# Expert routing on 64 candidate sums in place of 256, with norm sums and side steps reordered

## The chip, the cores and the metric

The kernel runs on one core of one Trainium2 chip. The metric is the device time of one execution in microseconds (us), the median of several runs. Durations of single instructions come from one profiled execution. Engines are called PE (matrix multiplication), DVE (vector), ACT (scalar), POOL (GpSimd) and SP (which issues DMAs).

## The reference, cut to what matters

A two-layer network over 256 tokens of width 1024, all in 32-bit floats. The first layer ends in a feed-forward part with product keys; the change is mostly there:

```
q = (ht @ w_q).reshape(T, PEER_HEADS, PEER_QDIM)
s1 = jnp.einsum('thd,nd->thn', q[..., :PEER_HALF], sub_k1)
s2 = jnp.einsum('thd,nd->thn', q[..., PEER_HALF:], sub_k2)
v1, i1 = lax.top_k(s1, PEER_TOPK)
v2, i2 = lax.top_k(s2, PEER_TOPK)
cand = (v1[..., :, None] + v2[..., None, :])      # 16 x 16 sums
cand_idx = (i1[..., :, None] * PEER_NKEYS + i2[..., None, :])
vals, pos = lax.top_k(cand, PEER_TOPK)
experts = jnp.take_along_axis(cand_idx, pos, axis=-1)
gates = jax.nn.softmax(vals, axis=-1)
```

There are 8 heads; each token and head chooses 16 of 128 x 128 = 16384 experts, whose rows `expert_u` and `expert_v` then weigh into the output. The kernel computes the products with all experts densely and masks them, so all of `expert_u` and `expert_v` streams through PE.

## The kernel before, in words

**Tiling.** Tokens are two tiles of 128 (`NT`). Weights come from HBM in blocks of 128 x 1024 floats (`w`, issued by SP). Each block is split into a high part on ACT (`whi`, line 298) and a low part on DVE (`wlo`, line 307), and a product is three matmuls (lines 408 to 410): one by the low part of the activations, one high by high, one by `wlo`. A block of `p_u`, `p_wq` or the like takes 24 matmuls of 256 columns.

**Buffers.** There are four buffers for `whi` and three for `wlo`; `prefetch` splits ahead as far as these reach. So a `wlo` may start only when PE has ended the block three before it, and DVE, which works in program order, stands still until then with all that is queued behind it.

**Side work.** Routing, norms and rotary steps are generators in the list `side`. After each block `tick` runs the steps that `after(n, f)` has put n ticks ahead, and then lets generators go on until `pace` credits are spent; a step costs what it yields (`STEP`, 650, where it yields nothing). `finish()` runs all that is left in `side` at once. The order of instructions on every engine is thus fixed when the program is written out.

**Routing.** `route` runs beside two stages: the query projection `p_wq` (16 blocks) and the first half of the experts' `p_u` (64 blocks, `u_pair`, outputs in `A1`). For each head and token tile `top16` chooses twice from 128 scores (lines 1227 to 1232: the best eight, their places, striking them out, and the same again), then POOL forms the 256 sums `cand` (line 1302), and `pick` chooses 16 of them. `keys(q)` turns the chosen places into indices of experts for four heads: `rr`, `rf` are row and column of the place, `eq` compares them with 0 to 15 (1024 wide), a product on POOL (line 1277) and a sum on DVE (line 1288) give `i1s`, `i2s`. `keys(0)` runs beside heads 5 to 7, `keys(1)` after the last head; behind it the gates are normalized (lines 1308 to 1314), and six transposes on PE (line 1320) bring indices and gates into place. The loop over `p_u` is followed by `finish()`.

**Norms.** `nm.columns` sums squares on PE (line 490) and starts the root (line 495 on DVE, 496 on POOL); `squares` and `diagonal` (502, 503, 514) prepare the matrix that PE spreads to rows (line 523).

**Second layer.** The attention pairs `pair_scores` and `full_flip` (lines 1753 and 1678) run with side steps of the last query slab (`q1`, `qkv_steps`); the pooling stage (line 2049) adds its products to `xT`.

Of the kernel before, what the change touches and what calls it, by code (L numbers as in the profile page):

```python
# [21 lines left out]
FT = mybir.dt.float32  # L22
# [128 lines left out]
def body(tc, a, out, dbg=None):  # L151
# [84 lines left out]
    with top:  # L236
# [419 lines left out]
        with b1:  # L656
# [37 lines left out]
            low_next()  # L694
            nm.square(2)
            nm.square(3)
            after(5, nm.squares)
            after(5, nm.diagonal)
            after(6, nm.rows)
            cb1 = ap_.tile([64, 512], FT, name="c_c_b1")  # L700
            cb2 = ap_.tile([16, 128], FT, name="c_c_b2")
# [124 lines left out]
                return evac_steps(lambda t, o: q_steps(name, dst, gain, t, o), ready[name])  # L826

            k_evac = evac_steps(k_steps, ready["ak"])
            kv_evac_ = evac_steps(kv_steps, ready["kk"])

            def kv_evac(t, o):
                if t == 0:
                    nm.columns()
                kv_evac_(t, o)

            def v_evac(t, o):
                S.activation(av[:, t], o, AF.Copy, scale=nm.rc[:, t:t + 1])
# [396 lines left out]

        KEYLAG = 8

        def route():
            def buf(dt, n):
                return [rp2.tile([128, 8, 16], dt, name=n, tag=n) for t in range(NT)]

            v12 = [buf(FT, f"v{e}") for e in range(2)]
            i12 = [buf(U32, f"i{e}") for e in range(2)]
            if12 = [buf(FT, f"if{e}") for e in range(2)]
            vals, pos = buf(FT, "vals"), buf(U32, "pos")
            last = [None, None]

            def pick(h, t):
                yield from top16(vals[t][:, h], pos[t][:, h], last[t].rearrange("p a b -> p (a b)"), 256)

            def keys(q):  # L1250

                hs, ks = ts(q, 4), ts(q, 64)
                for t in range(NT):
                    for e in range(2):
                        V.tensor_copy(if12[e][t][:, hs], i12[e][t][:, hs])
                    rr = rp2.tile([128, 2, 64], U32, name="rr", tag="rr", bufs=1)
                    rf = rp2.tile([128, 2, 64], FT, name="rf", tag="rf", bufs=2)
                    pf = pos[t][:, hs].rearrange("p h k -> p (h k)")
                    V.tensor_scalar(rr[:, 0], pf, 4, None, op0=OP.logical_shift_right)
                    V.tensor_scalar(rr[:, 1], pf, 15, None, op0=OP.bitwise_and)  # L1260
                    V.tensor_copy(rf, rr)
                    V.tensor_tensor(ig[2][:, t, ks].rearrange("p (h k) -> p h k", h=4), vals[t][:, hs],
                                    vals[t][:, hs, 0:1].to_broadcast([128, 4, 16]), op=OP.subtract)
                    yield
                    for e in range(2):
                        eq = rp2.tile([128, 4, 16, 16], FT, name="eq", tag="eq", bufs=2)
                        ef = eq.rearrange("p h k r -> p (h k) r")
                        args = (ef, rf[:, e, :, None].to_broadcast([128, 64, 16]), iota[:, None, 0:16].to_broadcast([128, 64, 16]))
                        if q == 0:

                            G.tensor_tensor(*args, op=OP.subtract)
                            S.activation(eq, eq, AF.Square)
                            S.activation(eq, eq, AF.Relu, scale=-1.0, bias=1.0)
                        else:
                            V.tensor_tensor(*args, op=OP.is_equal)
                            yield 1200
                        G.tensor_tensor(eq, eq, if12[e][t][:, hs, None, :].to_broadcast([128, 4, 16, 16]), op=OP.mult)
                        yield 1 if q == 0 else None
                        if q == 0:
                            w = 8  # L1280
                            while w > 1:
                                G.tensor_tensor(ef[:, :, 0:w], ef[:, :, 0:w], ef[:, :, w:2 * w], op=OP.add)
                                w //= 2
                            G.tensor_tensor(ig[e][:, t, ks, None], ef[:, :, 0:1], ef[:, :, 1:2], op=OP.add)
                            for _ in range(KEYLAG):
                                yield 1
                        else:
                            V.tensor_reduce(ig[e][:, t, ks], ef, axis=AX.X, op=OP.add)
                            yield 1200

            for h in range(8):
                while heads[0] <= h:
                    yield
                if h == 5:
                    spawn(keys(0))
                for t in range(NT):
                    for e in range(2):
                        yield from top16(v12[e][t][:, h], i12[e][t][:, h], sc[t][:, h, e], 128)
                    if h:
                        yield from pick(h - 1, t)  # L1300
                    last[t] = rp2.tile([128, 16, 16], FT, name="cand", tag="cand")
                    G.tensor_tensor(last[t], v12[0][t][:, h, :, None].to_broadcast([128, 16, 16]),
                                    v12[1][t][:, h, None, :].to_broadcast([128, 16, 16]), op=OP.add)
            for t in range(NT):
                yield from pick(7, t)
            yield from keys(1)

            S.activation(ig[2], ig[2], AF.Exp)
            gs = rp2.tile([128, 2, NT * 8], FT, name="gs", tag="gs", bufs=1)
            gall = ig[2].rearrange("p t (h k) -> p (t h) k", k=16)  # L1310
            V.tensor_reduce(gs[:, 0], gall, axis=AX.X, op=OP.add)
            V.tensor_scalar(gs[:, 0], gs[:, 0], 1.0 / GATE, None, op0=OP.mult)
            V.reciprocal(gs[:, 1], gs[:, 0])
            V.tensor_tensor(gall, gall, gs[:, 1, :, None].to_broadcast([128, NT * 8, 16]), op=OP.mult)
            yield
            yield
            g3 = [bank("tp"), bank("tp")]
            for i in range(3):
                for t in range(NT):
                    tr(g3[i // 2][:, ts((i % 2) * 2 + t)], ig[i][:, t], ident)  # L1320
            for i in range(2):
                V.tensor_copy(ib[i], g3[0][:, ts(i, T)])
            yield

            gT = g3[1][:, 0:T]
            V.tensor_copy(gp2[0], gT)
            V.tensor_tensor(gp2[1], gT, gp2[0], op=OP.subtract)

        pace[0] = 1 * STEP
        after(4, nm.columns)  # L1330
        after(5, nm.diagonal)
        after(6, nm.rows)
# [24 lines left out]
        def u_pair(c):  # L1357
            u_leave(c, u_products(c))

        pace[0] = 1200  # L1360
        o = u_products(0)
        head_scores(7)
        rs.close()
# [252 lines left out]
        with ExitStack() as es:  # L1616
            yp = pool(es, "y", side="right")
            y = yp.tile([128, 4, 512], FT, name="y")
            ws = [get("p_v", 126), get("p_v", 127, more=False)]

            def last_mm(q):
                h, t = divmod(q, 2)
                for k in range(2):
                    v_mm(126 + k, ws[k], t, (h,))

            def leave(q):
                if q == 1:
                    V.tensor_scalar(y[:, q], acc[q], 1.0 / GATE, None, op0=OP.mult)
                else:
                    S.activation(y[:, q], acc[q], AF.Copy, scale=1.0 / GATE)  # L1630

            def turned(h):
                o = [bank("tp") for _ in range(2)]
                for t in range(NT):
                    for i in range(4):
                        tr(o[i // 2][:, (i % 2) * T + t * 128:(i % 2) * T + (t + 1) * 128], y[:, 2 * h + t, ts(i)], ident)
                for k in range(2):
                    add(2 * h + k, o[k])

            for q in range(3):  # L1640
                last_mm(q)
                leave(q)
            turned(0)
            last_mm(3)
            leave(3)
            nm.operand(0)
            nm.operand(1)
            prefetch(3)
            filled(1)
            turned(1)  # L1650
            nm.operand(2)
            prefetch(2)
            nm.operand(3)
            prefetch(3)
            last_squares(nm)

        def full_scores(s, stk, scale, bufs):
# [25 lines left out]
        with at:  # L1683
# [82 lines left out]
            for pr in range(8):  # L1766
                if pr == 3:
                    finish(slab_steps[1])
                if pr < 7:
                    ss = pair_scores(pr + 1)  # L1770
                pts = []
# [8 lines left out]
                if pr < 7:  # L1780
                    pp = pair_probs(ss, pr + 1)
                if pr == 0:
                    q1.unit(3)

                kfs[0].tag = "s" if pr in (1, 2) else "mm"
                filled(FILL["pairs"][pr])
# [225 lines left out]
        with pm:  # L2012
# [23 lines left out]
            for gp_ in range(2):  # L2036
                w = get("pool", gp_)
                for q in range(2):
                    g = 2 * gp_ + q
                    o = bank()  # L2040
                    for d in range(2):
                        for k in range(2):
                            c0 = (2 * q + k) * 256 + d * 128
                            mm3(o[:, ts(d, T)], cut(w, ALL, slice(c0, c0 + 128)), cut(mT, ALL, 2 * g + k), k == 0, k == 1)
                    if g >= 2:
                        prefetch()
                    for d in range(2):
                        c = 2 * g + d
# [69 lines left out]
```

## Time and profile before

| | us |
|---|---|
| median of 3 runs (1732.07 to 1736.66) | 1734.8 |
| the profiled execution | 1734.57 |
| its span in the trace | 1732.8 |
| PE busy in the span | 1706.4 |
| DVE busy | 1377.5 |
| ACT busy | 941.9 |
| POOL busy | 164.4 |

PE is busy nearly all the time, so the few stretches in which it waits, or runs at a lower granted clock, are what side work can change. The span leaves 1.8 us of the profiled execution outside; the profiled execution stands 0.2 us below the median. Ends of matmuls are modelled, and two that follow each other overlap in the records: a matmul of 256 columns shows 0.28 us, while the next starts 0.12 us after it.

### The profile page before, as it was taken

To read this page: it belongs to the slowest core of one execution; us is meant where nothing else is said; L and a number is where in the kernel's file an instruction comes from. 1 tells how busy PE (TensorE), PEld (TensorE's weight loads), DVE (VectorE), ACT (ScalarE), POOL (GpSimd) and SP (SyncE) were. 2 spreads that over 40 slices of the span, in tenths; PEclk is the share of its full clock that TensorE was granted. 3 is DMA by queue.
4 is the path that set the end of the run, shared out by engine and by line. 5 is a ranking of instruction groups with operands and counts; after the bars stand their busy time and mean duration, and the time that the engine had idled before them with its cause. 6 is when DMAs were issued, how large, how long until landed. Compare 5 with 4: busy or idle time off the path is not lost. (4 is left out here: it accounts for less than half of the span.)

```text
span 1732.8 us, 31970 instructions
## 1 busy us (share of the span) xinstructions
PE 1706.4 (98%) x12658; PEld 1559.9 (90%) x12658; DVE 1377.5 (79%) x2440; ACT 941.9 (54%) x1399; POOL 164.4 (9%) x123
## 2 busy tenths in 40 slices
PE   9999999999999999999999999999999999999998
PEld 8977999999999998888888888689999999899997
DVE  6888879999877887898766658876788877678786
ACT  6556556445544444444454555665666666556664
POOL 1210020155200000000010001010200001020000
PEclk9999999999999999999999999999999999999999
DMA  6633455555655555555655655244656554455653
GB/s 233 204 119 101 135 177 176 188 169 170 197 177 167 168 169 183 170 171 169 216 190 187 195 165 183 86 146 134 198 184 204 186 179 157 135 188 192 188 189 122
DMA packets 83238, 297.66 MB, mean 172 GB/s; under 512 B 9280, under 2 KB 10320, under 8 KB 82960
## 3 DMA queue, kind: packets, MB, share of 16 engines
q1 hardware_dynamic: 81360, 291.68, 52.0%
q0 software_dynamic: 608, 2.62, 0.4%
q8 instruction: 99, 1.62, 0.4%
q10 hardware_dynamic: 1120, 1.32, 0.2%
q14 instruction: 51, 0.42, 0.1%
HBM read 294.54 MB, written 1.05 MB: 171 GB/s over the span
## 5 line engine op out<-in xcount | busy, mean ns | idle before, releaser
L298 ACT ACTIVATE whi<-w 128x1024 fp32r<-128x1024 f32 x537 | 566.1, 1057 | 437.2 <-PE s L1476 160.4
L307 DVE TENSOR_TENSOR wlo<-w,whi 128x1024 fp32r<-128x1024 f32 x537 | 682.7, 1276 | 129.7 <-issue 52.7
L410 PE MATMUL s<-hT,wlo 128*128 128x256 f32 x1024 | 286.7, 280 | 3.3 <-DVE wlo L307 3.2
L408 PE MATMUL s<-hT,whi 128*128 128x256 f32 x1024 | 287.4, 281 | 0.0
L409 PE MATMUL s<-hT,whi 128*128 128x256 f32 x1024 | 286.2, 280 | 0.0
L1476 PE MATMUL mm<-whi,hT 128*128 128x512 f32 x762 | 234.9, 389 | 0.0
L410 PEld LDWEIGHTS s<-hT,wlo 128*128 128x128 f32 x1024 | 191.9, 187 | 4.7 <-DVE wlo L307 4.6
L408 PEld LDWEIGHTS s<-hT,whi 128*128 128x128 f32 x1024 | 192.2, 188 | 0.0
L409 PEld LDWEIGHTS s<-hT,whi 128*128 128x128 f32 x1024 | 192.1, 188 | 0.0
L1476 PEld LDWEIGHTS mm<-whi,hT 128*128 128x128 f32 x762 | 143.0, 188 | 30.1
L1476 PE MATMUL mm<-wlo,hT 128*128 128x512 f32 x381 | 129.7, 394 | 0.0
L408 PE MATMUL mm<-hT,whi 128*128 128x256 f32 (+1 forms) x360 | 102.7, 285 | 0.0
L410 PE MATMUL mm<-hT,wlo 128*128 128x256 f32 (+1 forms) x360 | 101.7, 283 | 0.0
L409 PE MATMUL mm<-hT,whi 128*128 128x256 f32 (+1 forms) x360 | 101.4, 282 | 0.0
L408 PE MATMUL tp<-xTl,whi 128*128 128x256 f32 x352 | 99.6, 283 | 0.0
L408 PE MATMUL s<-xTl,whi 128*128 128x256 f32 x352 | 98.9, 281 | 0.0
L409 PE MATMUL s<-xTh,whi 128*128 128x256 f32 x352 | 98.8, 281 | 0.0
L410 PE MATMUL s<-xTh,wlo 128*128 128x256 f32 x352 | 98.8, 281 | 0.0
L410 PE MATMUL tp<-xTh,wlo 128*128 128x256 f32 x352 | 98.8, 281 | 0.0
L409 PE MATMUL tp<-xTh,whi 128*128 128x256 f32 x352 | 98.8, 281 | 0.0
L1476 PE MATMUL s<-whi,hT 128*128 128x512 f32 x254 | 98.5, 389 | 0.0
L397 DVE TENSOR_TENSOR hT<-A,hT 128x512 fp32r<-128x512 f32 (+1 forms) x64 | 44.0, 688 | 61.1 <-ACT hT L396 60.5
(478 smaller groups left out, 3957.9 us busy)
## 6 DMA issues: line engine op xcount, KB each, us to landing
w<-in_p_u_dram SPq DMA_DIRECT2D x128, 512.0 KB, 3.3
w<-in_p_v_dram SPq DMA_DIRECT2D x128, 512.0 KB, 3.4
w<-in_f_up_dram SPq DMA_DIRECT2D x88, 512.0 KB, 3.3
w<-in_f_down_dram SPq DMA_DIRECT2D x44, 512.0 KB, 3.9
w<-in_p_wq_dram SPq DMA_DIRECT2D x16, 512.0 KB, 3.3
w<-in_x_k_dram SPq DMA_DIRECT2D x16, 512.0 KB, 3.6
w<-in_x_v_dram SPq DMA_DIRECT2D x16, 512.0 KB, 3.4
w<-in_x_q_dram SPq DMA_DIRECT2D x16, 512.0 KB, 3.5
```

The lines of the kernel that those rows point to most:

```text
L298: S.activation(hi[:, c], w[:, c], AF.Copy)
L307: V.tensor_sub(lo[:, c], w[:, c], hi[:, c].bitcast(FT))
L397: V.tensor_sub(lo, src, hi.bitcast(FT))
L408: mm(o, l[0], r[1], start=start, stop=False, **kw)
L409: mm(o, l[0], r[0], start=False, stop=False, **kw)
L410: mm(o, l[1], r[0], start=False, stop=stop, **kw)
L1476: mm(acc[2 * h + t], l[k], w[m][:, ts(h, 512)], start=c == 0 and k == 0 and m == 1, stop=c == 127 and k == 1)
```

## The change

1. **64 sums.** With both lists sorted, a sum at row a and column b can be among the best 16 only where (a+1)(b+1) is at most 16. `cand` now holds four rectangles of the 16 x 16 table (`STAIRS`: row 0 with 16 columns, rows 1 to 3 with 8, rows 4 to 7 with 4, rows 8 to 15 with 1), 64 places, formed by four POOL instructions; `pick` runs over 64. `keys` must turn a place among 64 into row and column, which takes ten more small DVE instructions for each of its four passes, and one more `yield`.
2. **Pace.** `pace` is 1000 in place of 650 in `p_wq`, and 720 in place of 1200 in `p_u`.
3. **First norm.** `columns` goes from the evacuation `kv_evac` to a tick later, ahead of `squares` and `diagonal`.
4. **Squares before attention.** `prefetch(3)` becomes `prefetch()`, so one more `wlo` is issued there.
5. **Attention pairs.** `pace` is 0 around `q1.unit(3)`, `STEP` until pair 3, and then `2 * STEP`.
6. **Pooling.** `prefetch()` is called for g = 3 alone, not for g = 2.

```diff
+            for f in (nm.columns, nm.squares, nm.diagonal):
+                after(5, f)
...
+        STAIRS = ((0, 1, 16, 0), (1, 4, 8, 16), (4, 8, 4, 40), (8, 16, 1, 56))
...
-                yield from top16(vals[t][:, h], pos[t][:, h], last[t].rearrange("p a b -> p (a b)"), 256)
+                yield from top16(vals[t][:, h], pos[t][:, h], last[t], 64)
...
+                    row = rf[:, 0]
+                    V.tensor_scalar(row, rw[:, 0], -1.0, 0.0, op0=OP.add, op1=OP.max)
+                    V.scalar_tensor_tensor(row, rw[:, 1], -6.0, row, op0=OP.add, op1=OP.max)
+                    V.scalar_tensor_tensor(row, rw[:, 2], -48.0, row, op0=OP.add, op1=OP.max)
...
+                    V.tensor_tensor(rf[:, 1], rw[:, 2], rw[:, 0], op=OP.subtract)
+                    yield
...
+                    last[t] = rp2.tile([128, 64], FT, name="cand", tag="cand")
+                    for i0, i1, m, p0 in STAIRS:
+                        G.tensor_tensor(last[t][:, p0:p0 + (i1 - i0) * m].rearrange("p (a b) -> p a b", b=m),
+                                        v12[0][t][:, h, i0:i1, None].to_broadcast([128, i1 - i0, m]),
+                                        v12[1][t][:, h, None, 0:m].to_broadcast([128, i1 - i0, m]), op=OP.add)
...
-        pace[0] = 1 * STEP
+        pace[0] = 1000
...
-        pace[0] = 1200
+        pace[0] = 720
...
-            prefetch(3)
+            prefetch()
...
+                    pace[0] = 0
                     q1.unit(3)
+                    pace[0] = STEP
...
-                    if g >= 2:
+                    if g == 3:
                         prefetch()
```

The rows below are the order in which instructions stand on an engine; numbers behind a name tell buffers apart, and the numbers of lines above 680 differ between the two kernels.

DVE at the kernel's first norm, before: `nst` at line 495 takes the sums from PE, and `qn` at line 760 is the rotary work on the first products.

```order
L484 TENSOR_TENSOR nacc<-nacc 128x256
L307 TENSOR_TENSOR wlo<-w,whi 128x1024
L495 TENSOR_SCALAR nst<-tp 128x2
L760 TENSOR_TENSOR qn<-mm,c_ghead 128x128 x4
L307 TENSOR_TENSOR wlo<-w,whi 128x1024
L502 TENSOR_SCALAR nst<-nst 128x2
L503 TENSOR_TENSOR nst<-nst 128x2
L514 TENSOR_TENSOR ndg<-first,nst 128x256
```

And after the change:

```order
L484 TENSOR_TENSOR nacc<-nacc 128x256
L307 TENSOR_TENSOR wlo<-w,whi 128x1024
L760 TENSOR_TENSOR qn<-mm,c_ghead 128x128 x4
L307 TENSOR_TENSOR wlo<-w,whi 128x1024
L495 TENSOR_SCALAR nst<-tp 128x2
L502 TENSOR_SCALAR nst<-nst 128x2
L503 TENSOR_TENSOR nst<-nst 128x2
L514 TENSOR_TENSOR ndg<-first,nst 128x256
```

`nst` of line 495, and with it POOL's root, has moved behind the four `qn` and a `wlo`. On PE the two matmuls of line 490 stand 24 matmuls (one block) later.

DVE at the end of the first half of `p_u`, before: the last token tile of `keys(1)` and the gates, from its first comparison to the casts of the transposed results.

```order
L1275 TENSOR_TENSOR eq_5606<-rf_5601,c_iota_2835 128x1024
L307 TENSOR_TENSOR wlo_5610<-w_5506,whi_5572 128x1024
L307 TENSOR_TENSOR wlo_5641<-w_5539,whi_5614 128x1024
L1288 TENSOR_REDUCE i1s_2837<-eq_5606 128x64
L307 TENSOR_TENSOR wlo_5674<-w_5570,whi_5645 128x1024
L1275 TENSOR_TENSOR eq_5704<-rf_5601,c_iota_2835 128x1024
L307 TENSOR_TENSOR wlo_5706<-w_5612,whi_5678 128x1024
L307 TENSOR_TENSOR wlo_5739<-w_5643,whi_5710 128x1024
L1288 TENSOR_REDUCE i2s_2838<-eq_5704 128x64
L307 TENSOR_TENSOR wlo_5770<-w_5676,whi_5743 128x1024
L1311 TENSOR_REDUCE gs_5801<-gts_2839 128x16
```

And after the change, from the last `wlo` ahead of the same work (between `i2s` of the first tile and the first `eq` here lie sixteen instructions 64 or 128 wide of lines 1252 to 1274):

```order
L307 TENSOR_TENSOR wlo_5957<-w_5865,whi_5931 128x1024
L1300 TENSOR_REDUCE i2s_2838<-eq_5923 128x64
...
L1287 TENSOR_TENSOR eq_6009<-rf_5994,c_iota_2835 128x1024
L1300 TENSOR_REDUCE i1s_2837<-eq_6009 128x64
L1287 TENSOR_TENSOR eq_6013<-rf_5994,c_iota_2835 128x1024
L1300 TENSOR_REDUCE i2s_2838<-eq_6013 128x64
L1327 TENSOR_REDUCE gs_6018<-gts_2839 128x16
L1328 TENSOR_SCALAR gs_6018<-gs_6018 128x16
L1329 RECIPROCAL gs_6018<-gs_6018 128x16
L1330 TENSOR_TENSOR gts_2839<-gts_2839,gs_6018 128x256
L1338 CAST ib0_2831<-tp_6023 128x256
```

Where six `wlo` stood between these steps, none stands now: they are written out in one piece by `finish()`.

PE at the same place, after the change: the last matmul of the block that uses `wlo_5893`, the transposes, and the first of the next block. (`wlo_5863` is used by the block before; `wlo_5957` takes its buffer.)

```order
L410 MATMUL s_5926<-hT_2840,wlo_5893 128x256
L1336 MATMUL tp_6023<-first_76,i1s_2837 128x128 x2
L1336 MATMUL tp_6023<-first_76,i2s_2838 128x128 x2
L1336 MATMUL tp_6024<-first_76,gts_2839 128x128 x2
L408 MATMUL s_6056<-hT_2840,whi_5897 128x256
L410 MATMUL s_6056<-hT_2840,wlo_5927 128x256
```

Before, the transposes stood three blocks (72 matmuls) earlier, inside the loop; now they stand behind its last block.

## Rows read from the trace of the kernel before

**Rows 1.** Page, part 1: busy us, share of the span, instructions.

```profile
PE 1706.4 (98%) x12658; PEld 1559.9 (90%) x12658; DVE 1377.5 (79%) x2440; ACT 941.9 (54%) x1399; POOL 164.4 (9%) x123
```

**Rows 2.** Timeline of PE, one block of p_u: start us, us, instruction.

```profile
453.91 0.28 PE L408 MATMUL s<-hT,whi 128*128 128x256 f32 x1
...
456.73 0.28 PE L408 MATMUL s<-hT,whi 128*128 128x256 f32 x1
```

**Rows 3.** Waits of PE over the span: us in total, times, longest us.

```profile
PE s L410 <- DVE wlo L307: 3.2, 4, 1.4
PE tp L490 <- DVE nacc L484: 2.1, 1, 2.1
PE s L1753 <- ACT fp L1664: 1.8, 3, 1.0
PE mm L408 <- DVE xT L2049: 1.2, 1, 1.2
...
PE mm L408 <- DVE wlo L307: 0.9, 1, 0.9
...
PE tp L1320 <- DVE gts L1314: 0.3, 1, 0.3
```

**Rows 4.** Windows: length, then busy (x) of PE, PEld, DVE, ACT, POOL, then PEclk.

```profile
21.60:23.20 1.60, 1.60 (x10) 1.60 (x9) 0.00 (x0) 1.44 (x3) 0.11 (x1) 0.51 0.92 246
23.20:25.00 1.80, 1.80 (x11) 1.80 (x10) 1.55 (x5) 1.80 (x5) 0.00 (x0) 0.50 0.26 100
```

**Rows 5.** Timeline at the first norm: start us, us, engine, line, [idle before <-releaser].

```profile
19.70 0.61 PE L490 MATMUL tp<-ones,nacc 128*128 128x2 f32 x4 [2.09 <-DVE nacc L484]
...
21.00 0.71 POOL L496 TENSOR_TENSOR nst<-nst,nhalf 128x2 f32<-128x2 f32 x1 [18.30 <-DVE nst L495]
...
24.35 1.22 DVE L307 TENSOR_TENSOR wlo<-w,whi 128x1024 fp32r<-128x1024 f32 x1
...
25.76 0.42 DVE L514 TENSOR_TENSOR ndg<-first,nst 128x256 f32<-128x256 f32 x1
...
27.50 0.61 PE L523 MATMUL tp<-ndg,ones 128*128 128x128 f32 x4
```

**Rows 6.** Timeline near the end of p_wq: a wlo, and its first use.

```profile
277.29 1.21 DVE L307 TENSOR_TENSOR wlo<-w,whi 128x1024 fp32r<-128x1024 f32 x1
...
279.92 0.28 PE L410 MATMUL s<-hT,wlo 128*128 128x256 f32 x1
```

**Rows 7.** Timeline in p_u: POOL's product, the wlo beside it, PE.

```profile
369.33 2.40 POOL L1277 TENSOR_TENSOR eq<-eq,if 128x1024 f32<-128x1024 f32 x1 [2.77 <-ACT eq L1273]
369.40 3.41 DVE L307 TENSOR_TENSOR wlo<-w,whi 128x1024 fp32r<-128x1024 f32 x1
...
372.87 0.39 PE L410 MATMUL s<-hT,wlo 128*128 128x256 f32 x1 [1.41 <-DVE wlo L307]
```

**Rows 8.** Groups of DVE by form: count, busy us, mean ns, idle before.

```profile
L1227 DVE MAX8 v<-sc 128x8 f32<-128x128 f32 x32 | 9.0, 280 | 0.0
...
L1227 DVE MAX8 vals<-cand 128x8 f32<-128x256 f32 x16 | 6.6, 413 | 0.0
...
L1275 DVE TENSOR_TENSOR eq<-rf,c_iota 128x1024 f32<-128x1024 f32 x4 | 4.9, 1216 | 0.0
...
L1255 DVE CAST if<-i 128x64 f32<-128x64 uint32 x8 | 1.1, 182 | 0.0
```

**Rows 9.** Timeline of DVE at the end of routing.

```profile
454.72 1.21 DVE L1288 TENSOR_REDUCE i2s<-eq 128x64 f32<-128x1024 f32 x1
...
457.57 0.42 DVE L1311 TENSOR_REDUCE gs<-gts 128x16 f32<-128x256 f32 x1 [0.51 <-ACT gts L1308]
...
458.52 0.42 DVE L1314 TENSOR_TENSOR gts<-gts,gs 128x256 f32<-128x256 f32 x1
```

**Rows 10.** Timeline of DVE in the attention pairs, first and last of six.

```profile
1093.96 0.69 DVE L1710 TENSOR_TENSOR qn<-qn,z 128x512 f32<-128x512 f32 x1
...
1096.74 0.23 DVE L639 TENSOR_SCALAR hst<-hst,nst 128x8 f32<-128x8 f32 x1
```

More of the change, by code (lines that the diff above doesn't have):

```diff
@@ L828, in body @@
             k_evac = evac_steps(k_steps, ready["ak"])
[L829 to L834, printed above, removed]
+            kv_evac = evac_steps(kv_steps, ready["kk"])
             def v_evac(t, o):
@@ L1256, in keys @@
                     rr = rp2.tile([128, 2, 64], U32, name="rr", tag="rr", bufs=1)
+                    rw = rp2.tile([128, 3, 64], FT, name="rw", tag="rw", bufs=1)
                     rf = rp2.tile([128, 2, 64], FT, name="rf", tag="rf", bufs=2)
                     pf = pos[t][:, hs].rearrange("p h k -> p (h k)")
-                    V.tensor_scalar(rr[:, 0], pf, 4, None, op0=OP.logical_shift_right)
-                    V.tensor_scalar(rr[:, 1], pf, 15, None, op0=OP.bitwise_and)
-                    V.tensor_copy(rf, rr)
+                    for i in range(2):
+                        V.tensor_scalar(rr[:, i], pf, 3 - i, None, op0=OP.logical_shift_right)
+                    V.tensor_copy(rw[:, 0:2], rr)
+                    V.tensor_copy(rw[:, 2], pf)
+                    row = rf[:, 0]
+                    V.tensor_scalar(row, rw[:, 0], -1.0, 0.0, op0=OP.add, op1=OP.max)
+                    V.scalar_tensor_tensor(row, rw[:, 1], -6.0, row, op0=OP.add, op1=OP.max)
+                    V.scalar_tensor_tensor(row, rw[:, 2], -48.0, row, op0=OP.add, op1=OP.max)
+                    V.tensor_scalar(rw[:, 0], row, 8.0, 8.0, op0=OP.mult, op1=OP.add)
+                    V.tensor_scalar(rw[:, 1], row, 4.0, 24.0, op0=OP.mult, op1=OP.add)
+                    V.scalar_tensor_tensor(rw[:, 0], row, 16.0, rw[:, 0], op0=OP.mult, op1=OP.min)
+                    V.scalar_tensor_tensor(rw[:, 1], row, 48.0, rw[:, 1], op0=OP.add, op1=OP.min)
+                    V.tensor_tensor(rw[:, 0], rw[:, 0], rw[:, 1], op=OP.min)
+                    V.tensor_tensor(rf[:, 1], rw[:, 2], rw[:, 0], op=OP.subtract)
+                    yield
                     V.tensor_tensor(ig[2][:, t, ks].rearrange("p (h k) -> p h k", h=4), vals[t][:, hs],
@@ L1300, in route @@
                         yield from pick(h - 1, t)
-                    last[t] = rp2.tile([128, 16, 16], FT, name="cand", tag="cand")
-                    G.tensor_tensor(last[t], v12[0][t][:, h, :, None].to_broadcast([128, 16, 16]),
-                                    v12[1][t][:, h, None, :].to_broadcast([128, 16, 16]), op=OP.add)
+                    last[t] = rp2.tile([128, 64], FT, name="cand", tag="cand")
[3 more added lines that the diff above has]
+                                        v12[1][t][:, h, None, 0:m].to_broadcast([128, i1 - i0, m]), op=OP.add)
             for t in range(NT):
@@ L1768, in body @@
                     finish(slab_steps[1])
+                    pace[0] = 2 * STEP
                 if pr < 7:
```

2 lines of the change are left out of this document (removed).

## The prediction

> **What bounds the kernel now.** I read first the page's busy shares: PE is busy for 1706.4 of 1732.8 us [rows 1], so what side work can still win is the 26 us in which PE stands, and what it can lose is any new stretch in which PE stands. The second view is the timeline of PE in one stage: in a block of `p_u` the same step recurs eight times in 456.73 - 453.91 = 2.82 us [rows 2], which is the time of one block and the unit in which all cover is counted below. The third view is the table of PE's waits [rows 3]: there the reader should see that it waits mostly for DVE, for a late `wlo`, and in pieces of 1 us or less apart from two. A wait's idle understates what it costs, since a matmul of 0.28 us in the records is followed after 0.12 when nothing waits; I add 0.16 to each. The fourth is the table of windows at the start [rows 4]: between 21.6 and 25.0 the granted clock is 0.51 and 0.50, the lower of its two levels (1.2 and 2.4 GHz), and this follows a wait of 2.09 us [rows 5].
>
> DVE's total is no measure here. What counts is where the program's order puts its work against PE's, since a `wlo` three blocks ahead of its use holds DVE until PE has ended the block whose buffer it takes.
>
> **The choice of 16 among 64.** The nearest rows are MAX8 over 128 (0.280 us) and 256 (0.413) [rows 8]: the slope of 0.133 for 128 places gives 0.21 for 64, half of 256. Finding and striking have the same widths, so of five passes each falls by about 0.2, 1.0 us a choice, 16 us for 16 choices. Against it, `keys` has ten more instructions on 64 elements, 0.18 each by the cast [rows 8], in four passes: 7 us. POOL's four small sums instead of one lie beside DVE's next choices, and only `pick`, a step later, reads them: nothing, and at most a tenth of a us each if that cover went. Off PE's path the net gain of 9 us is worth what PE's waits in that stage are. These are four late `wlo`, 3.2 us, and the gates, 0.3 [rows 3], with 0.16 for each 4.3 in all. The longest shows the cause: POOL's product of 2.40 us beside which a `wlo` takes 3.41 instead of 1.21, and PE then waits 1.41 [rows 7]. At 720 credits a tick DVE reaches the buffers' limit in this stage and such a delay is taken up by the lead. I take **-4.3** (bounds -4.3 and 0).
>
> **The pace in the query projection.** With 1000 credits in place of 650 more choices are put ahead of each `wlo`. By the order of the two programs, ahead of the `wlo` that starts at 277.29 there are two more choices from 128 (1.44 each) and one more from the sums (1.1): 4.0 us. That `wlo` ended at 278.50 and was first used at 279.92 [rows 6]: 1.4 us of slack. So PE waits 4.0 - 1.4 = **+2.6** there (0 if DVE found gaps the order does not show, 4.0 if no slack is left).
>
> **The end of the first half.** This is the largest term. In `p_u` a tick now spends 720 credits instead of 1200, while the steps of `keys(1)` cost what they did, and one `yield` more each. By the order they don't end within the loop, and `finish()` writes out the rest at once: behind `wlo_5957` DVE has no `wlo` until the gates are done, and PE's transposes, now behind the loop's last block, wait for it. Both start from the end of the block that used `wlo_5863`. DVE then needs, by durations of before: the `wlo` 1.2; the last sum `i2s` of the first tile 1.2 [rows 9]; sixteen small instructions at 0.18, less where they overlap, 2.6; comparison 1.2 [rows 8], POOL's product 2.4 [rows 7], sum 1.2; the same three again, 4.8; the gates from 457.57 to 458.94, 1.4 [rows 9]. Together 1.2 + 1.2 + 2.6 + 4.8 + 4.8 + 1.4 = 16.0. PE has one block to do meanwhile, 2.8. It stands for **+13.2**. If small instructions cost half and hand-overs overlap, 11; with POOL's product at 3.4 and full small instructions, 15.5. Two more blocks have their `wlo` ready after that, 5.6 us, and the next is made within it, so nothing follows from DVE.
>
> What does follow is the clock. In the trace a wait of 2.09 us was followed by 3.4 us at half clock, 1.7 us lost [rows 4, 5]. After 13 us I take the same, **+1.7** (0 to 3.4).
>
> The Trainium skill, "VectorE: DVE Perf Modes", section "The TRN2 errata", gives every vector instruction a fixed extra of 58 cycles, so many small ones are dear, a rule that speaks against the longer `keys`; by its formula one of 64 elements takes 0.13 us, an estimate, against 0.18 in the cast's row. By that figure the sixteen would take 2.0 in place of 2.6, and PE would stand 12.6. The row decides.
>
> **The first norm.** `nst` of line 495 moves behind four `qn` and a `wlo`. PE no longer waits 2.09 us for the sums, and does two blocks at once; but the spread at 27.50 [rows 5] needs `ndg`. In the new order: `wlo` ends at 25.57, `nst` 0.1, POOL's root 0.71 with hand-overs of 0.2, lines 502 and 503 0.3, `ndg` 0.42: 27.4. PE, which stopped at 19.70 - 2.09 = 17.61, gets there two blocks later, by some 23.4, and stands 4.0 us; the gain is 0.1. But the half clock that now covers waiting time (PE would otherwise be early) falls after 27.4, on work that nothing hides: 1.7. I take **+1.5** (-0.3 to +2).
>
> **The three small moves.** Ahead of the attention, one `wlo` stood behind a norm's sum; PE waited 0.9 [rows 3]. It is now made ahead of that sum; the `wlo` behind it follows closely, so I don't take all of 0.9 + 0.16: **-0.8** (-1.1 to 0). In the pairs, six DVE instructions from 1093.96 to 1096.97 [rows 10] move behind the scores' work; of the 1.8 us in three waits for `fp` [rows 3], 2.3 with the 0.16 each, most goes, and the second slab's transposes come nearer to their use: **-1.8** (-3 to 0). In pooling PE waits 1.2 for `xT` [rows 3] behind two `wlo`; one moves behind it: **-1.3** (-1.4 to 0).
>
> **Sum.** -4.3 + 2.6 + 13.2 + 1.7 + 1.5 - 0.8 - 1.8 - 1.3 = +10.8. From the profiled 1734.6 (0.2 below the median) that is 1745.4.
>
> **Rivals.**
> *The choices win.* DVE is what PE waits for in both routing stages; it is 9 us lighter, and if the last pass of `keys` is covered after all (it would have to start six blocks, 17 us, before the loop's end, or PE to have other ready work), the terms without the end, the clock there and the wait in the projection are -4.3 + 1.5 - 0.8 - 1.8 - 1.3 = -6.7: 1727.9, faster. It decides from the point where PE stands less than 4.1 us at the transposes. For it: DVE's busy share of 79% leaves room. Against it: the order has no `wlo` there, and no block.
> *It cancels.* The end is half covered, 6 to 7 us in place of 15, because small instructions and POOL's products are quicker than in the rows of before, and the rest stands: about 1737.
> *The clock stays low longer.* After each of the two long waits half clock lasts twice as long as in rows 4, 3.4 us lost at each: 1745.4 + 1.7 + 1.9 = 1749. The Trainium skill, "TensorE: Matmul & The Clock Gate", section "HAM oscillation", says that a gap between bursts returns the engine to half rate and that the next burst starts cold. In rows 4 and 5 the low clock shows from 21.6, 1.9 us after PE went on at 19.70, so the trace has a fall behind a wait, but a burst that starts cold is shown by no row here.
>
> **How the numbers follow.** The forecast, with the terms at their values or near, 0.57; the clock low for longer 0.21; the end half covered 0.11; the choices win 0.11. The predicted time is 1745.4. Its own range is 1740 to 1750, from the bounds of the end (11 to 15.5), the projection (0 to 4.0) and the clock. To leave out no more than 2 in 10 I take 1734 to 1751, which holds the second rival and the third, and leaves out the first. A measurement of this kernel can tell 0.3% from no change, 5.2 us: slower is above 1740.0, 0.80; within 1729.6 to 1740.0, 0.10; faster 0.10.
>
> **What would show it.** In the profile after: PE's wait for the transposes of line 1336 should head the waits, 11 to 15 us in one piece, with DVE at `eq`, POOL's product and sum in turn and no `wlo`; windows behind it should show 0.5 of granted clock for some us; the waits for `wlo` in `p_u` should be gone, with DVE idle there for PE; at the start a wait of 3 to 4 us at line 523 in place of that at 490. It would be wrong if the transposes' wait is under 5 us, if PE waits in `p_u` for reasons that the order doesn't show, or if POOL's small sums, four times as many, are late for `pick`.

## The result, and the profile after

The changed kernel takes 1745.56 us (median of 4 runs, 1744.23 to 1746.25) against 1734.55 before: a ratio of 1.0066, with a 95% interval of 1.0051 to 1.0081. The forecast was 1745.4. Its profiled execution took 1744.23 us with a span of 1742.4, which is 9.6 more than the span before. One run of an experiment below (`e9_mix950`, 5951.5 us, the other eleven at most 1737.4) is left out of its comparison.

Page, part 1, of the changed kernel (busy us, share, instructions), to be held against [rows 1]:

```profile
PE 1708.1 (98%) x12658; PEld 1563.1 (90%) x12658; DVE 1371.7 (79%) x2480; ACT 942.3 (54%) x1399; POOL 170.3 (10%) x171
```

DVE is busy 5.8 us less, and PE has the same number of matmuls. The difference must be time in which PE stood or ran slowly. PE's waits after (us in total, times, longest), which answer to [rows 3]:

```profile
PE tp L1336 <- DVE i1s L1300: 7.4, 1, 7.4
PE tp L1336 <- DVE i2s L1300: 4.2, 1, 4.2
PE tp L1191 <- DVE qTl L397: 2.4, 3, 1.1
PE s L408 <- DVE xkl L397: 1.9, 1, 1.9
...
PE tp L1336 <- DVE gts L1330: 0.9, 1, 0.9
...
PE s L1769 <- ACT aqT L649: 0.7, 1, 0.7
```

Three waits in one place, at the transposes of line 1336, make 12.5 us, where the kernel before had 0.3. The waits for `wlo` in `p_u`, 3.2 us before, are gone from the list, and so is the one for the norm's sums.

Since PE executes nearly the same matmuls in the same order, the start of the same matmul in both traces tells where time went. The steps below are how much the distance between the two starts grew in a stage (times of before; the span's growth is their sum):

| stage, us of before | what is in it | forecast | measured |
|---|---|---|---|
| 0 to 28.7 | first norm | +1.5 | -3.2 |
| 28.7 to 249.5 | first layer's attention part, start of the projection | 0 | +1.1 |
| 249.5 to 281.3 | projection, `qTl` late | +2.6 | +2.5 |
| 281.3 to 437.0 | `p_u`, `wlo` late | -4.3 | -5.0 |
| 437.0 to 1031.8 | end of the first half, and its clock | +14.9 | +14.7 |
| 1031.8 to 1067.8 | squares | -0.8 | -0.1 |
| 1067.8 to 1183.3 | attention pairs | -1.8 | +0.5 |
| 1183.3 to 1477.9 | pooling | -1.3 | -0.9 |
| sum | | +10.8 | +9.6 |

**The end of the first half.** Timeline of DVE there, after (start us, us, instruction, idle before it and what ended it):

```profile
464.62 1.22 DVE L1287 TENSOR_TENSOR eq<-rf,c_iota 128x1024 f32<-128x1024 f32 x1
468.35 1.22 DVE L1300 TENSOR_REDUCE i1s<-eq 128x64 f32<-128x1024 f32 x1 [2.52 <-POOL eq L1289]
469.49 1.22 DVE L1287 TENSOR_TENSOR eq<-rf,c_iota 128x1024 f32<-128x1024 f32 x1
473.22 1.22 DVE L1300 TENSOR_REDUCE i2s<-eq 128x64 f32<-128x1024 f32 x1 [2.52 <-POOL eq L1289]
...
475.30 0.42 DVE L1330 TENSOR_TENSOR gts<-gts,gs 128x256 f32<-128x256 f32 x1
...
478.10 1.22 DVE L307 TENSOR_TENSOR wlo<-w,whi 128x1024 fp32r<-128x1024 f32 x1
```

DVE and POOL take turns, there is no `wlo` until 478.10, and the gates end at 475.72. The last sum of the first tile began at 460.80, so with a `wlo` of 1.2 ahead of it the piece took 16.1 us; the prediction had 16.0. PE, in the same stretch:

```profile
469.63 0.48 PE L1336 MATMUL tp<-first,i1s 128*128 128x128 f32 x1 [7.39 <-DVE i1s L1300]
469.90 0.42 PE L1336 MATMUL tp<-first,i2s 128*128 128x128 f32 x1
474.50 0.48 PE L1336 MATMUL tp<-first,i2s 128*128 128x128 f32 x1 [4.18 <-DVE i2s L1300]
475.87 0.66 PE L1336 MATMUL tp<-first,gts 128*128 128x128 f32 x2 [0.90 <-DVE gts L1330]
```

From start to start these three steps cost 13.3 us (7.6, 4.5 and 1.3 over the usual). Then the windows behind them (length; busy and count of PE, PEld, DVE, ACT, POOL; granted clock; DMA share; GB/s):

```profile
475.00:477.00 2.00, 1.13 (x6) 1.16 (x7) 1.77 (x5) 0.00 (x0) 0.00 (x0) 0.50 0.00 0
477.00:479.00 2.00, 2.00 (x11) 2.00 (x11) 1.98 (x7) 0.00 (x0) 0.00 (x0) 0.50 0.00 0
479.00:481.00 2.00, 2.00 (x11) 2.00 (x11) 0.32 (x1) 0.00 (x0) 0.00 (x0) 0.50 0.28 61
481.00:485.00 4.00, 4.00 (x34) 4.00 (x33) 2.27 (x3) 1.44 (x2) 0.00 (x0) 0.94 0.52 165
```

PE goes on at 475.87 at the lower level (1.2 GHz) and reaches the upper one some 0.5 us after 481: 5.6 us at half clock, 2.8 lost. Here the burst does start cold, as the Trainium skill ("TensorE: Matmul & The Clock Gate", "HAM oscillation") says. 13.3 + 2.8 is 16.1; the stage came out at 14.7, since the gates' wait of before (0.5 with its overlap) is gone and some 0.7 us comes back between 495 and 527, by an effect that the last section tells.

**The first norm.** PE's spread, and ACT's split of the first block of `w_mg`, after:

```profile
18.62 1.06 ACT L298 ACTIVATE whi<-w 128x1024 fp32r<-128x1024 f32 x1 [0.50 <-DMA w<-in_w_mg_dram]
...
24.23 0.68 PE L523 MATMUL tp<-ndg,ones 128*128 128x128 f32 x4 [0.52 <-DVE ndg L514]
```

The spread came at 24.23 and not at 27.4, with a wait of 0.5 us and not of 4, and no half clock behind it. The weights landed earlier, which experiment 1 takes up. The profile of before also has 3.4 us of half clock here [rows 4], and that is not a fixed part of the old order: experiment 4 has the same order at this place, with a wait of 2.0 us at the sums and the full clock behind it:

```profile
19.75 0.61 PE L490 MATMUL tp<-ones,nacc 128*128 128x2 f32 x4 [1.99 <-DVE nacc L484]
```

```profile
22.00:24.00 2.00, 2.00 (x19) 2.00 (x18) 1.93 (x7) 1.07 (x2) 0.00 (x0) 1.00 0.76 258
```

Its stage to 28.7 is 1.4 us shorter than that of before, and `w_mg` landed there 3.9 us after its issue, as in the changed kernel. So by these profiles, of the 3.2, 1.4 is the half clock of the one execution of before, and 1.8 the new order's at an early landing.

### The profile page after: what moved, and what is told of

Read it like the earlier page. It is cut to its first block, busy times and chain, and to the rows that moved or that the text cites. A ratio compares the mean times of both kernels' runs of the same rounds, so it can differ in the third digit from the quotient of the medians.

```text
span 1742.4 us, 32057 instructions
## 1 busy us (share of the span) xinstructions
PE 1708.1 (98%) x12658; PEld 1563.1 (90%) x12658; DVE 1371.7 (79%) x2480; ACT 942.3 (54%) x1399; POOL 170.3 (10%) x171
## 5 line engine op out<-in xcount | busy, mean ns | idle before, releaser
L1371 ACT ACTIVATE A<-s 128x512 f32<-128x512 f32 x64 | 38.3, 598 | 101.7 <-PE s L410 101.7
```

What stands on the lines that cost most here:

```text
L1371: S.activation(A[h][:, cc:cc + 2], pairs(o), AF.Gelu_apprx_tanh)
```

## The experiments

The experiments ran in three groups, each on one chip together with the kernel before. The medians of before were 1734.15 us beside experiments 1 to 4, 1733.16 beside 5, 6, 8 and the first mixture of 9, and 1735.06 beside 7 and the second mixture; differences are taken within a group.

**1. The first norm alone** (`e4_first_norm`): the kernel before with

```diff
-            after(5, nm.squares)
-            after(5, nm.diagonal)
+            for f in (nm.columns, nm.squares, nm.diagonal):
+                after(5, f)
...
-                if t == 0:
-                    nm.columns()
```

> The kernel before, with the norm columns of the first norm moved and nothing else. By the prediction's step: 1.5 us longer, since PE waits some 4 us at the spread and the half clock falls behind it. By the rival that the trace after suggests (the spread is ready when w_mg lands, and it landed 3.9 us after issue there instead of 6.6): PE waits 0.5 to 0.7 us at the spread, no half clock, 2 to 3.5 us shorter where the weights land early; the profile should show the landing of w_mg beside the wait.

Measured: 1731.42 us (9 runs) against 1734.15, a ratio of 0.9983 (0.9971 to 0.9996): 2.7 us shorter by the medians, with an interval of 0.7 to 5.0. Its profile, however, shows the kind of thing that the prediction described, a wait at the spread (2.2 us, not 4.0) with half clock behind it, and at 38 us it is 0.2 us behind the profile of before. The spread, two windows behind it, and then the landing of `w_mg` (issues, KB each, us from issue to landing):

```profile
26.16 0.68 PE L523 MATMUL tp<-ndg,ones 128*128 128x128 f32 x4 [2.21 <-DVE ndg L514]
```

```profile
27.00:29.00 2.00, 2.00 (x14) 2.00 (x13) 1.93 (x6) 1.61 (x3) 0.70 (x1) 0.65 0.26 65
29.00:31.00 2.00, 2.00 (x11) 2.00 (x11) 1.93 (x9) 0.00 (x0) 1.03 (x1) 0.50 0.77 228
```

```profile
w<-in_w_mg_dram SPq DMA_DIRECT2D x1, 512.0 KB, 6.0
```

The same row reads 6.6 in the profile of before and 3.9 in that of after:

```profile
w<-in_w_mg_dram SPq DMA_DIRECT2D x1, 512.0 KB, 6.6
```

```profile
w<-in_w_mg_dram SPq DMA_DIRECT2D x1, 512.0 KB, 3.9
```

So the spread's time follows this landing, and the landing varies from one execution to the next. Here `w_mg` was issued at 14.49 and had landed at 20.5, in the changed kernel it was issued at 14.59 and had landed at 18.5, and the spread began 5.7 us later in both; in all ten profiles with the new order it is 5.7 us. Over the profiles with the new order, a landing of 3.9, 4.3, 4.6, 4.8, 4.9, 5.3, 5.6, 5.8, 6.0 and 6.2 us goes with a wait at the spread of 0.5, 0.8, 0.8, 1.6, 1.3, 1.6, 1.9, 2.1, 2.2 and 2.2; half clock followed in two of them (landings of 5.8 and 6.0). In the two profiles with the old order, with landings of 6.6 and 3.9, PE waits 2.1 and 2.0 us for the sums. The prediction took one execution's late landing, 6.6 us, for the rule.

**2. The pace in `p_u` back at 1200** (`e1_u1200`), the changed kernel with

```diff
-        pace[0] = 720
+        pace[0] = 1200
```

> The changed kernel, with the pace in the first half of p_u put back from 720 to 1200. Theory (what is left of routing at the end of the loop is written out in one piece and PE stands for it): the transposes return into the loop, PE's wait of 13 us at them and the half clock behind it go, so about 13.5 + 2.7 = 16 us less than the changed kernel, 1729 to 1730. With 64 places a tick's choices are shorter, so the late wlo of p_u may come back in part, up to 2 us. Rival (the longer keys work on DVE and POOL is itself what costs, wherever it stands): the time stays above 1740.

Measured: 1749.27 us (4 runs) against 1734.15, a ratio of 1.0082 (1.0057 to 1.0107), so no faster than the changed kernel with its 1.0066. The wait at the transposes did go, down to 1.7 us. But PE now waits in `p_u`, and three rows show how one such wait comes about:

```profile
PE s L410 <- DVE wlo L307: 13.3, 11, 3.1
```

```profile
364.52 1.94 POOL L1283 TENSOR_TENSOR eq<-rf,c_iota 128x1024 f32<-128x1024 f32 x1 [4.66 <-DVE rf L1265]
364.58 1.93 DVE L1268 TENSOR_SCALAR rw<-rf 128x64 f32<-128x64 f32 x1
...
368.49 0.58 PE L410 MATMUL s<-hT,wlo 128*128 128x256 f32 x1 [3.06 <-DVE wlo L307]
```

Both theories fail as they stood: the expected 1729 is 20 us off, and the longer `keys` don't cost wherever they stand, since at 720 `p_u` shows no wait at all. What follows is that at a pace of 1200 DVE can't take 64 places with the longer `keys`, though it took 256 with the shorter. Two things come together. The first is the credits. A choice from 128 costs 1090 credits and takes 1.43 us; one from 256 costs 1730 and takes 2.1; one from 64 costs 770 and takes 1.10 in this trace. A head and token tile (two choices from 128 and one of the sums) is 4.96 us for 3910 credits before, 1.27 us for 1000, and 3.96 us for 2950 now, 1.34 for 1000. At 1200 a tick that is 1.52 and 1.61 us; with a `wlo` of 1.22 it makes 2.74 and 2.83, against the 2.82 of a block [rows 2]. The traces have it a little longer: from one `wlo` to the next DVE takes 2.77 us on average before (24 blocks from 282.39), and 2.92 here (15 blocks from 285.26). So here DVE loses its lead ahead of `keys(0)`, at the cost of one wait of 0.4 us.

The second is a step of `keys`, and the greater part of the waits stands beside it. A step is charged 650 credits where it yields nothing, and the first step of a pass now holds fifteen small instructions in place of six:

```profile
330.26 0.29 DVE L1252 CAST if<-i 128x64 f32<-128x64 uint32 x2
...
332.03 1.95 DVE L1269 SCALAR_TENSOR_TENSOR rw<-rf,rw 128x64 f32<-128x64 f32 x1
...
334.41 0.22 DVE L1272 TENSOR_TENSOR rf<-rw 128x64 f32<-128x64 f32 x1
...
335.83 0.39 PE L410 MATMUL s<-hT,wlo 128*128 128x256 f32 x1 [2.33 <-DVE wlo L307]
```

That step takes 4.3 us here, although it costs fewer credits than one choice, and the blocks with such a step in `keys(0)` last 5.4 and 6.3 us from one `wlo` to the next, against 2.8 and 2.5 before. Behind them PE waits 2.3 and 3.1 us, its two longest; most of the others stand beside other work of `keys`. One of the small instructions (0.19 us elsewhere) took 1.93 beside POOL's comparison. So the rival was right in part: without DVE's lead the longer `keys` do cost. The Trainium skill, "GPSIMD Engine Reference", section "Key points", has this contention for DVE instructions with two inputs or in a mode with two ports; the rows agree for the `wlo` of 3.41 in [rows 7], which has two inputs. For the instruction of 1.93, which has one, no row shows the mode.

The same stretch of 60 us in the changed kernel, and then here:

```profile
300.00:360.00 60.00, 60.00 (x512) 60.00 (x511) 48.15 (x152) 28.04 (x32) 8.59 (x21) 1.00 0.54 183
```

```profile
300.00:360.00 60.00, 55.27 (x452) 54.15 (x451) 58.04 (x209) 27.87 (x33) 29.26 (x44) 0.97 0.48 166
```

With DVE busy for 48 us PE never stands; with DVE busy for 58 PE does 60 matmuls fewer of 512, by 4.7 us of standing and a spell of half clock behind one of the waits (granted clock 0.97 in the mean).

**3. Both old paces** (`e2_old_paces`): the same, and 650 in place of 1000 in the projection.

> The changed kernel, with both paces of before (650 in the projection, 1200 in p_u): 64 places without the new paces. Theory: as the run with 1200 alone, and the waits for qTl at the end of the projection (2.8 us in the changed kernel, 0.5 before) go as well: 1727 to 1728. Rival (those waits come from the order of other steps, not from the pace): the same time as with 1200 alone.

Measured: 1744.48 us (4 runs). The part on the projection holds: the stage from 249.5 to 281.3 is 0.3 us shorter than before, where the changed kernel has +2.5, and 1744.48 is 4.8 below experiment 2, of which that stage has 2.8. The part on `p_u` falls as above: its waits for `wlo` are 12.8 us. So with the paces of before, 64 places and the other moves are 10 us slower than before (a ratio of 1.0053, 1.0036 to 1.0069).

**4. The new paces on 256 places** (`e3_paces_256`): the kernel before with 1000 and 720.

> The kernel before, with the two new paces and nothing else, so still 256 places. Theory: with longer choices more is left over at the loop's end, some 34 us of DVE and POOL work of which PE's one block covers 2.8: PE stands for about 31 us there, half clock costs 2.7 more, the projection costs 2 to 3, and most of the 4.3 us of late wlo go; 1765 to 1770. Rival (the wait at the end comes from the 64 places and their longer keys): no long wait at the transposes, within 5 us of the kernel before.

Measured: 1768.41 us (2 runs), as expected. PE's waits, first two rows:

```profile
PE tp L1320 <- DVE i1s L1288: 27.3, 2, 17.2
PE tp L1320 <- DVE i2s L1288: 4.2, 1, 4.2
```

So the wait at the end does not come from the 64 places, which shorten it; it comes from what the pace leaves over. The stage of `p_u` is 5.0 us shorter than before here too, with 256 places, and no `wlo` is late in it.

**5. A smaller rest** (`e6_u780`): the changed kernel with 780 in place of 720.

> The changed kernel with the pace in p_u at 780. Behind the last wlo now stand one sum, one comparison, POOL's product, a sum and the gates: 1.2 + 1.2 + 1.2 + 2.4 + 1.2 + 1.4 = 8.6 us, less one block of 2.8. Theory: PE stands 5.8 us at the transposes in place of 13, with up to 2 us of half clock behind it; 1736 to 1739. Rival (the wait at the end has another cause than the work written out there): the wait stays above 10 us or is gone.

Measured: 1738.83 us (10 runs) against 1733.16. PE at the transposes:

```profile
464.09 0.33 PE L1336 MATMUL tp<-first,i1s 128*128 128x128 f32 x1 [1.51 <-DVE i1s L1300]
464.26 0.27 PE L1336 MATMUL tp<-first,i2s 128*128 128x128 f32 x1
468.96 0.48 PE L1336 MATMUL tp<-first,i2s 128*128 128x128 f32 x1 [4.43 <-DVE i2s L1300]
470.33 0.66 PE L1336 MATMUL tp<-first,gts 128*128 128x128 f32 x2 [0.90 <-DVE gts L1330]
```

6.8 us of idle where 5.8 were expected. With one comparison, product and sum less behind the last `wlo`, and the small instructions too, the wait falls from 12.5 by 5.6. The half clock behind it lasts to 476.2 and costs some 2.9 us, where up to 2 were expected.

**6. No rest but the gates** (`e5_u850`): 850.

> The changed kernel with the pace in p_u at 850 in place of 720. In the order of the program the last comparisons of keys then stand between wlo, and only the gates (1.4 us) are written behind the last one. Theory (two costs of one number: too low and the rest is written out at the end, too high and choices of 64, which cost more than their credits, make wlo late): the wait at the transposes goes with its half clock, 13.3 + 1.3 to 2.7 less, and DVE still keeps up: 1730 to 1733. Rival (at any pace without a rest at the end the wlo of p_u come late, as at 1200): over 1738.

Measured: 1730.93 us (10 runs) against 1733.16, a ratio of 0.9993 (0.9979 to 1.0007). The time is the expected one, but the wait is not gone: 3.5 us are left, all for the gates, with half clock behind them.

```profile
466.83 0.66 PE L1336 MATMUL tp<-first,gts 128*128 128x128 f32 x2 [3.47 <-DVE gts L1330]
```

By the sum there should be none, since only 1.4 us of DVE work stand behind the last `wlo`, under a block of 2.8. What is left is a chain through ACT, which neither the prediction nor the expectation has: the exponential of the gates stands on ACT behind the step that takes the loop's last products, and that step waits for PE itself.

```profile
462.96 0.60 ACT L1371 ACTIVATE A<-s 128x512 f32<-128x512 f32 x1 [0.83 <-PE s L410]
463.57 1.28 ACT L1324 ACT_TABLE_LOAD   x1
464.86 0.42 ACT L1324 ACTIVATE gts<-gts 128x256 f32<-128x256 f32 x1
```

DVE's gates begin behind it at 465.31, and no block covers any of this. In the changed kernel the same chain ends at 465.2, long before DVE's rest, and doesn't show. That the time met its range is in part luck: 3.7 us in this execution come from the shorter pitch of the last section.

From 720 to 850, 18% of one number, the kernel goes from 11 us slower than before to a difference that can't be told from none.

**7. The projection's pace alone** (`e10_wq650`): the changed kernel with 650 there.

> The changed kernel with the pace of 650 in the projection alone. By the prediction's step the 2.5 to 2.6 us of late qTl go there; by the step on the end, less routing done early leaves more for the end: behind the last wlo stand one more sum and one more comparison with POOL's product, 4.8 us, so PE stands about 18 there instead of 13. Together 1747 to 1749. If the waits for qTl are not the pace's doing, the projection stays as it is.

Measured: 1746.47 us (2 runs). The projection's stage is 0.3 us shorter than before, and the rest at the end grew as expected:

```profile
473.81 0.47 PE L1336 MATMUL tp<-first,i1s 128*128 128x128 f32 x1 [12.11 <-DVE i1s L1300]
...
478.68 0.47 PE L1336 MATMUL tp<-first,i2s 128*128 128x128 f32 x1 [4.18 <-DVE i2s L1300]
480.05 0.66 PE L1336 MATMUL tp<-first,gts 128*128 128x128 f32 x2 [0.90 <-DVE gts L1330]
```

With 0.65 ahead of these, 17.8 us where 18 were expected. The time is 0.5 below the range expected. By the profiles the pace of 1000 in the projection thus pays 2.5 us there and gets 5.4 back at the end; of this difference of 2.9 the medians show 0.4 (11.4 above before, against 11.0), with two runs here.

**8. The pairs without their pace** (`e7_no_pairs`): the changed kernel with

```diff
-                    pace[0] = 2 * STEP
...
-                    pace[0] = 0
                     q1.unit(3)
-                    pace[0] = STEP
```

> The changed kernel without its change of pace in the attention pairs. By the prediction's step the pairs cost 1.8 us more than with it; by the stage table of the trace after, where the stage came out 0.5 us longer than before, they cost 0.5 us less. The profile decides by the stage between the squares and the pooling, the whole time hardly: 1745 to 1748 by the one, 1744 to 1746 by the other.

Measured: 1744.65 us (3 runs), 11.5 above its own before, so nothing that can be told from the changed kernel's 11.0. The stage of the pairs is 0.9 us longer than before here and 0.5 in the changed kernel; but both hold a spell of half clock that the profile of before does not. One window of each, first without the pace, then the changed kernel:

```profile
1113.00:1115.00 2.00, 2.00 (x8) 1.35 (x8) 1.79 (x2) 1.72 (x4) 0.00 (x0) 0.50 0.58 225
```

```profile
1114.00:1116.00 2.00, 2.00 (x12) 2.00 (x11) 1.97 (x5) 0.49 (x2) 1.48 (x1) 0.50 0.15 61
```

Experiments 6 and 7 have the changed pairs without such a spell, and there the stage is 0.4 us shorter than before. So the move is worth about 0.4 where no half clock follows. Half clock comes in executions of either order, in five of the seven profiles with the changed pairs and in two of the other five, and costs more than that; whether the move gains anything in the median is not shown.

**9. Mixtures.** `e8_mix`: 64 places, 650 in the projection, 900 in `p_u` and 1200 from the start of `keys(1)`, the pairs of before, and the rest of the change.

> 64 places with the pace of 650 in the projection, 900 in p_u and 1200 from the start of keys(1), the first norm, the squares and the pooling of the changed kernel, and the pairs of the kernel before. By the terms measured so far: first norm -2.7, p_u's late wlo -4.3, pooling -0.9, no wait at the end and none in the projection: 1725 to 1728. If choices at 900 still make wlo late, up to 4 us more, 1730.

Measured: 1730.5 us (12 runs) against 1733.16, a ratio of 0.9982 (0.9967 to 0.9996). This is above the 1725 to 1728 expected, at the 1730 named for late `wlo`; they are 1.3 us, the wait at the transposes 2.2.

`e9_mix950`: all of the change, with 650, 950, and 1200 from the start of `keys(1)`.

> All of the change, with the pace at 650 in the projection, 950 in p_u and 1200 from the start of keys(1). In the order the transposes then stand three blocks ahead of the loop's end, as before, with wlo between all steps of keys. If choices at 950 leave DVE within a block (about 1.25 + 1.28 = 2.53 of 2.82 us), neither a wait at the transposes above 1 us nor late wlo are left: 1728 to 1730. If they come late as at 1200, 1732 to 1736.

Measured: some 1734 us (11 runs) against 1735.06, a ratio of 0.9994 (0.9981 to 1.0006), within the range for late `wlo`. These are back with 5.3 us, five times, and the transposes wait 1.4. The choices are not what makes them late: ahead of `keys(0)` no `wlo` is late and DVE mostly has some idle time in each block, as the 2.53 of 2.82 us said. All five stand behind work of `keys`, the first (1.5 us) behind a block of 6.0 us with the fifteen small instructions, the second (1.6) behind a `pick` that waits 3.1 us for its sums, since POOL is still at `keys(0)`. Between 720 and 1200 a pace trades the wait at the end for late `wlo`; a higher price for that step of `keys`, or more yields in it, was not tried. The best of the mixtures is no better than experiment 1, which leaves routing as it was.

## Why the prediction was right, and where only its sum was

**Right in mechanism and size: the end of the first half.** Of the +10.8 it carried 14.9, and 14.7 was measured. The piece took 16.1 us where 16.0 were summed, and PE stood for 13.3 where 13.2 were expected, though in three pieces and not in one; experiments 4, 5 and 7 move it with the amount of work that the order leaves behind the last `wlo` (32.4, 6.8 and 17.8 us of idle where the changed kernel has 12.5). Only the 3.5 us of experiment 6 have another cause, ACT's chain. The half clock behind it was under-sized: 2.8 us where 1.7 were taken, inside the bounds.

**Right: the projection and `p_u`.** 2.5 us of waits for `qTl` where 2.6 us were expected, though at other instructions than the `wlo` that the working named; experiments 3 and 7 show that the pace makes them. In `p_u` all late `wlo` went, 5.0 us where 4.3 were taken; since experiment 4 has the same 5.0 with 256 places, this is the work of the lower pace and not of the lighter choices. The size of a choice among 64 held too: MAX8 took 0.214 us against the 0.21 from the slope.

**Wrong: the first norm.** +1.5 was forecast, -3.2 measured in the profile (1.4 of it the half clock of the profile of before), and -2.7 by medians in experiment 1. The failed step is "`wlo` ends at 25.57": that was read from a trace in which `w_mg` had landed 6.6 us after its issue, and the chain behind it was taken as fixed. It landed after 3.9 to 6.2 in the others. The length of the chain was right: 5.7 us behind a landing as late as that of before (15.09 + 6.59 = 21.68) is the 27.4 of the prediction. The wait of 4.0 was too long even so, since PE got to the spread at 23.4 to 24.7 in the ten profiles and not always by 23.4; the longest wait was 2.2. The half clock behind a long wait at the spread, which the step added, appears in two profiles of the ten with the new order.

**Wrong: the pairs.** -1.8 was forecast, +0.5 measured. The waits for `fp` did fall, from 1.8 to 0.4 us; 1.9 for `xkl` and 0.7 for the slab's transposes took their place, where before had 1.0 and none. The failed step is that most of the 2.3 us goes: what PE would wait for next had no term, and without half clock the gain is 0.4 (experiments 6 and 7). The step had no term either for the half clock that followed in this execution.

**Smaller.** The squares' wait of 0.9 came back as one of 0.5 for the next `wlo`, 2.6 us later, and one for `z` grew from 0.5 to 0.65, so -0.1 where -0.8 was taken. Pooling gave 0.9 of the 1.3. POOL's sums, which were to cost nothing, were late for `pick` once in the changed kernel, by 0.9 us of DVE's time and at no cost to PE, since `p_u` shows no wait. The reading that all pieces of PE's waits but two are 1 us or less was off, since [rows 3] has three longer ones (2.1, 1.4 and 1.2), but nothing rests on it.

**The rivals.** "The choices win" was the case only from the point it named: in experiment 6, where PE stands 3.5 us, the time is below before by 2.2 us, too little to tell from none, and no more than the first norm alone gives in experiment 1. No run here shows that 64 places themselves make the kernel faster. Its sum of 6.7 us of gains was not reached there: squares and pairs gave 0.7 of their 2.6, and the projection's 2.5, which it leaves out, are still in. "It cancels" failed, since PE stood 13.3 us and not 6 to 7. "The clock stays low longer" came nearer than the forecast at the end (2.8 us lost, where it had 3.4 and the forecast 1.7), and was wrong for the first norm.

So the total met the forecast to 0.2 us, but that is chance: terms of 4.7 too much (first norm), 2.3 too little (pairs) and 1.1 not foreseen at all (between 28.7 and 249.5) cancel with the smaller misses in part, and the profiled execution itself lies 1.3 below the median.

## What to carry to other kernels

Where side work is doled out by a budget a tick, its rest has a place too: look in the program's order at what stands behind the last piece of main work, sum it on the engines that take turns, and subtract the cover; that sum held here to 0.1 us, and to 1.4 us in experiments 4, 5 and 7. Where it comes out at nothing, look at what no block covers: work that starts from the loop's last product, as ACT's did in experiment 6. When the pieces get smaller, the budget's prices must be checked again, since a fixed part of an instruction makes short ones dearer than their price, and the same budget then overfills a tick; a price for each step, whatever it holds, is worse still (here 650 for a step of 4.3 us). And of a DMA's landing one trace shows one draw: before a chain is built on it, ask what the term becomes if it lands as early as the other landings of its kind in that trace.

## What the runs showed of the hardware that was not expected

**Two pitches at one granted clock.** Matmuls of 256 columns follow each other after 118 ns in most stretches and after 113 in others, both at a granted clock of 1.00, and a stretch can last tens of microseconds. The same work, 20 us of it, before and after:

```profile
210.00:230.00 20.00, 20.00 (x178) 20.00 (x178) 16.69 (x20) 13.36 (x20) 4.76 (x3) 1.00 0.64 205
```

```profile
207.00:227.00 20.00, 20.00 (x173) 20.00 (x171) 16.45 (x20) 12.93 (x19) 4.41 (x2) 1.00 0.60 202
```

178 matmuls against 173, with no idle in either. The kernel before had the shorter pitch there from 207 to 237 and the changed one did not: this is the +1.1 of the table's second row. Of the ten other profiles seven have it there and three don't, with the same order on PE. After the end of the first half, the changed kernel has it from 495 to 527 (some 0.7 us gained), experiments 4 and 6 for over 100 us (some 4.2 and 3.7 us gained). What sets it was not tried and stays open.

**Half clock after waits of 2 us is a matter of the execution.** The same wait of about 2 us at the spread was followed by it in two profiles (2.1 and 2.2 us of wait), not in others (1.9, and 2.2 in experiment 7). The wait of 1.9 us for `xkl` in the pairs was followed by it in five of the seven profiles that have it, among them the changed kernel, and not in experiments 6 and 7. In all twelve profiles nine of fifteen waits between 1.85 and 2.33 us were followed by it, and every wait of 3.06 us and more.
